# Orders of work at five places of a hybrid decoder layer: opening, key heads, MoBA's last head, third token tile, last parts of w_down

## Chip, cores and metric

The kernel runs on one core of a Trainium2 chip. The metric is the device time of one execution in microseconds (us), the median of several runs; less is better. The engines have short names: PE is TensorE (PEld its weight loads), DVE is VectorE, ACT is ScalarE, POOL is GpSimd, and SP issues most of the DMAs.

## What is computed

One layer of a decoder for 512 tokens and 1024 columns, all in float32. The width of the feed-forward part is 4096.

```python
def reference(x, p, w_in, ...):
    u = rms_norm(h, attn_pre_norm)
    gq, gk, gv, gz, gb, ga, mq, mk, mv = split(u @ w_in)
    o_gdn = gated_deltanet_group(gq, gk, gv, gz, gb, ga, conv_w, ...)   # 4 heads of 128
    o_moba = moba_group(mq, mk, mv, positions)                         # 4 heads of 128
    mix = concatenate([o_gdn, o_moba]) @ w_out
    h = h + rms_norm(mix, attn_post_norm)
    f = square(relu(rms_norm(h, mlp_pre_norm) @ w_up)) @ w_down
    h = h + rms_norm(f, mlp_post_norm)
    return h + sigmoid(h @ w_ple_gate) * (p @ w_ple)
```

The delta-rule heads (GDN) run a short convolution and SiLU over q, k and v, norm q and k, and work in chunks. A MoBA head is causal softmax attention of tiles of 128 queries; with two blocks of 256 every past block is selected.

## The kernel before

**Splitting.** Every large product is computed with operands split into a high and a low half: ACT casts the source to the high half (`L169`, `L209`, `L236`, `L749`), DVE subtracts it from the source to give the low half (`L170`, `L210`, `L237`, `L750`), and PE does three matmuls for each pair (`mm3`, `L193`). So each weight and each activation passes ACT and then DVE before PE can use it.

**Order.** Each engine runs its own queue in order. Between `L240` and `L342` (the opening) the queues of ACT, DVE and PE are in the order of the code (`tc.manual_schedule`); everywhere else a scheduler orders them by readiness and priority. SP's queue is ordered by the scheduler throughout. An instruction that waits holds up those behind it on its engine, though they may be ready.

**Opening.** The four token tiles of `x` are squared on ACT (`squares`), a root is taken on POOL, DVE scales (`normed`), PE transposes (`transpose_in`, tiles `ut`, with two PSUM buffers), and ACT and DVE split the result into `uTh` and `uTl`. Between these stand the products of `p` with `w_ple` (`embed`), whose results are copied out of PSUM (`keep`) and stored to DRAM as `ple`, and the first weight chunks `wv0` to `wv3`. `project` is the first large projection.

**Key heads.** For each of the four GDN heads `proj_conv(1, h, ...)` projects and convolves the keys into `kF`; `key_head(h)` multiplies `kF` with itself (`pkk`), transposes it (`ptk`) and computes the triangle whose inverse is then solved on DVE (`M`, from `L489`). `gdn_head(0)` follows with the queries (`pc`, `qF`, `pkq`).

**MoBA's last head.** `moba_head(3)` computes for four query tiles the scores `sc`, their softmax (`pr`; DVE scales it by the reciprocal of its sum at `L656`), the transposes `prt` on PE and the product with the values. At the same time `finish(2)` and `finish(3)` norm the outputs `u` of the last GDN heads: POOL takes a power for `so` (`L154`), DVE multiplies it (`L636`), ACT scales `u` (`L638`), and PE transposes `u` into `pot` during the gate projection `pz`.

**Third token tile.** In the loop over tiles at `L791`, the out projection of a tile (`po`) is normed, added to `x` (`L805`), and scaled (`L809`) into `xr`, from which the transposes `u2` of the next stage are made; their split is `u2Th` and `u2Tl`. The transposes of tile `t - 2` stand in the middle of tile `t`'s projection (`L798`). The first `up` products (`pu`) follow.

**The feed-forward part.** Blocks of `w_up` are multiplied (`up`, tiles `pu`), and their output goes through ReLU and square into `f`; each `f` has two sides. Three of the four groups use seven products for eight (`product`, tiles `pd`); the last group's `f` is kept split in `f_hl` (`L852`), and its parts of `w_down` are loaded and split one after another (`load_split`, `L940`), then multiplied for each token tile in `L965` and onward. Slabs of one tile row (`sf` for sources, `sr` for split halves) are taken from the front of a list and given back to its end:

```python
        def take(self):
            return self.free.pop(0)
        def give(self, *slabs):
            self.free.extend(slabs)
```

`sr.more(R_LATE, dr_)` adds twelve new slabs at the end of the list once the earlier buffers are closed. A slab's former reader must be done before it is written anew, and an instruction that waits for that holds up its queue.

Of the kernel before, what the change touches and what calls it, by code (L numbers as in the profile page):

```python
# [9 lines left out]
F32 = mybir.dt.float32  # L10
# [5 lines left out]
P = 128  # L16
# [53 lines left out]
def hybrid_layer(ctx: ExitStack, tc: tile.TileContext, x, p, w_in, w_tok, w_out, w_up, w_down, w_ple, w_gate,  # L70
# [136 lines left out]
    def put_split(dst, src):  # L207

        nc.scalar.copy(dst[0], src)  # L209
        nc.vector.tensor_sub(dst[1], src, dst[0].bitcast(F32))  # L210

    def transpose_in(u, dst, t, name, ahead=0):

        for q in range(2):
            pt = ptr(f"{name}{t}_{q}")
            for i in range(4):
                k = 4 * q + i
                nc.tensor.transpose(pt[:, i * P:(i + 1) * P], u[:, k * P:(k + 1) * P], ident)
            s = (slice(None), slice(4 * q, 4 * q + 4), slice(t * P, (t + 1) * P))
            with tc.high_priority(ahead):  # L220
                put_split((dst[0][s], dst[1][s]), j4(pt))
# [18 lines left out]
    opening = tc.manual_schedule(engines={mybir.EngineType.Activation, mybir.EngineType.DVE, mybir.EngineType.PE})  # L240
# [41 lines left out]
    def split_wv(t):  # L282
        hi, lo = split_raw(wv_raw[t], 2, 520, f"wv{t}")
        wv.extend((hi[:, i, :], lo[:, i, :]) for i in range(2))
# [53 lines left out]
    split_wv(2)  # L338
    normed(3)
    split_wv(3)  # L340
# [44 lines left out]
    def proj_conv(c, h, y):  # L385
        f = c * 4 + h
        w = load_chunk(w_in[f], P, f"w{c}{h}")
        pm = pmm(f"pc{c}{h}")
        for k in range(KT):
            mm3(pm, w[k], (uT[0][:, k, :], uT[1][:, k, :]), k == 0, k == KT - 1)  # L390
        nc.scalar.activation(y, pm, AF.Copy, scale=conv_w[:, f, 3:4])
        for i in (1, 2, 3):
            nc.vector.scalar_tensor_tensor(y[:, i:], pm[:, :T - i], conv_w[:, f, 3 - i:4 - i], y[:, i:],
                                           op0=ALU.mult, op1=ALU.add)

        th = g.tile([P, T], F32, tag="F", bufs=3, name=f"th{c}{h}")
        nc.scalar.activation(th, y, AF.Tanh, scale=0.5)
        nc.vector.scalar_tensor_tensor(y, th, 1.0, y, op0=ALU.add, op1=ALU.mult)
# [80 lines left out]
    for h in range(H):  # L479
# [5 lines left out]
        if h:  # L485
            key_head(h)


    M = g.tile([64, 2, BLK, BLK], F32, tag="M", bufs=1, name="M")  # L489
    N_, V_ = M[:, 0], M[:, 1]  # L490
    flat = lambda ap: ap.rearrange("p r c -> p (r c)")
    nc.gpsimd.memset(flat(V_), 0.0)
    nc.gpsimd.memset(flat(V_)[:, ::BLK + 1], 1.0)
    nc.sync.dma_start(flat(N_), scr.rearrange("u b r c -> (u b) (r c)"))
    for k in range(BLK - 1):
        a, b = k + 1, BLK - 1 - k
        tm = g.tile([64, a, b], F32, tag="tm", bufs=2, name=f"tm{k}")
        nc.vector.tensor_mul(tm, V_[:, :a, k:k + 1].to_broadcast([64, a, b]), N_[:, k:k + 1, a:].to_broadcast([64, a, b]))
        nc.vector.tensor_sub(V_[:, :a, a:], V_[:, :a, a:], tm)
    nc.sync.dma_start(scx[0].rearrange("u b r c -> (u b) (r c)"), flat(V_))  # L500
    nc.scalar.copy(N_.rearrange("p r c -> p c r"), V_)
    nc.sync.dma_start(scx[1].rearrange("u b r c -> (u b) (r c)"), flat(N_))
    for i in (1, 0):
        for b in range(4):
            s = slice(b * BLK, (b + 1) * BLK)
            nc.sync.dma_start(XX[i][s, :, s], scx[i, :, b].rearrange("u r c -> r u c"))
# [4 lines left out]
    def gdn_head(h):  # L511
        qf = g.tile([P, T], F32, tag="qF", bufs=3, name=f"qF{h}")
        proj_conv(0, h, qf)
# [45 lines left out]
    gdn_head(0)  # L559
# [69 lines left out]
    def finish(h):  # L629
# [6 lines left out]
        nc.vector.scalar_tensor_tensor(s, s, 0.5, rq, op0=ALU.mult, op1=ALU.mult)  # L636
# [3 lines left out]


    def moba_head(h):
        PT = g.tile([P, 4, T], F32, tag="M", bufs=1, name=f"PT{h}")
        for i in range(4):
# [11 lines left out]
            nc.vector.tensor_scalar(pr[:, :N], pr[:, :N], sum_, None, op0=ALU.mult)  # L656
# [20 lines left out]
    finish(2)  # L677
    finish(3)
# [112 lines left out]
    for t in range(NT):  # L791
# [16 lines left out]
        for i in range(2):  # L808
            nc.vector.scalar_tensor_tensor(xr[:, hf(i)], h_t[t][:, hf(i)], r, nw[1][:, hf(i)], op0=ALU.mult, op1=ALU.mult)  # L809
        nc.sync.dma_start(hd[tk(t), :], h_t[t])  # L810
        give(h_t[t])
# [21 lines left out]
    def up(b, c0, c1, between=None):  # L833
# [115 lines left out]
    give(S_s, *(sums[i] for i in (1, 7, 4)))  # L949
    C = ((sums[2], sums[3]), (sums[6], sums[5]))  # L950
# [103 lines left out]
```

## Time and profile before

| | us |
|---|---|
| median of 3 runs | 688.68 (688.54 to 688.79) |
| the profiled execution | 688.31 |
| its span on the engines | 686.5 |
| PE busy | 675.6 (98%) |
| DVE busy | 442.9 (65%) |
| ACT busy | 322.9 (47%) |
| POOL busy | 38.8 (6%) |
| granted clock of PE | 0.999 of full speed |

Times in the trace start at 0 with the span. The start of a matmul is observed, its end is modelled, so successive matmuls overlap in the rows; the distance of their starts is what one costs. The value in brackets at the end of a row is the idle time of the engine before it and what ended that.

### The profile page before, as it was taken

The numbers are of one execution on the slowest core, as the hardware profiler recorded it, in microseconds if no ns is written. First come the engines' busy times: TensorE is split into PE (matmuls) and PEld (weight loads), VectorE is DVE, ScalarE is ACT, GpSimd is POOL, SyncE is SP. The second block draws the span as 40 slices with busy tenths as digits, with TensorE's granted clock in tenths as the row PEclk, the third lists the DMA queues.
The fourth block names the chain that finished last, engine by engine and source line by source line (L and its number), as shares of the span: only waits on it lengthen the run. The fifth ranks groups of instructions, "written<-read, shape, count | busy, mean of one in ns | idle before, by whom it ended". The sixth has DMA issues, their size and how long they took to land.

```text
span 686.5 us, 8997 instructions
## 1 busy us (share of the span) xinstructions
PE 675.6 (98%) x3418; PEld 563.2 (82%) x3418; DVE 442.9 (65%) x708; ACT 322.9 (47%) x597; POOL 38.8 (6%) x72
## 2 busy tenths in 40 slices
PE   8999999999999999999999999999999999999997
PEld 6998888888877768899888888888888888788886
DVE  5759889367676655776286356956678758556632
ACT  6535343433566654555265644444444445512411
POOL 1301100000001000120000000000000000011000
PEclk9999999999999999999999999999999999999999
DMA  8831323532011117477004340154301033632431
GB/s 328 314 124 62 104 87 103 116 114 93 32 32 62 32 63 264 164 260 262 32 31 151 126 153 32 37 179 140 105 32 61 32 123 110 213 92 61 137 109 47
DMA packets 37980, 79.24 MB, mean 115 GB/s; under 512 B 9712, under 2 KB 10352, under 8 KB 37936
## 3 DMA queue, kind: packets, MB, share of 16 engines
q1 hardware_dynamic: 37360, 77.60, 34.5%
q10 hardware_dynamic: 576, 1.05, 0.5%
q8 instruction: 27, 0.44, 0.3%
q14 instruction: 17, 0.14, 0.1%
HBM read 70.51 MB, written 7.08 MB: 113 GB/s over the span
## 4 chain that ended last, share of the span: by engine, by line
PE 88%; DVE 3%; DMA 3%; ACT 2%; issue 2%; POOL 1%; ACTq 0%; DVEq 0%; POOLq 0%
PE pu L197 16%; PE pd L197 14%; PE pu L194 8%; PE pd L194 7%; PE pc L197 5%; PE pg L197 4%; PE pc L194 3%; PE po L197 3%; PE wv L197 2%; PE pg L194 2%; PE pmk L197 2%; PE pmq L197 2%; PE pz L197 2%; DMA sf<-in_w_down 1%; PE po L194 1%
## 5 line engine op out<-in xcount | busy, mean ns | idle before, releaser
L197 PE MATMUL pd<-sr,sr 128*128 128x512 f32 x464 | 143.5, 390 | 0.7 <-DVE sr L750 0.7
L197 PE MATMUL pu<-u2Tl,sr 128*128 128x512 f32 (+1 forms) x288 | 105.3, 366 | 0.5 <-DVE u2Tl L210 0.5
L194 PE MATMUL pu<-u2Th,sr 128*128 128x512 f32 (+1 forms) x288 | 105.4, 366 | 0.0
L197 PE MATMUL pu<-u2Th,sr 128*128 128x512 f32 (+1 forms) x288 | 105.2, 365 | 0.0
L197 PEld LDWEIGHTS pd<-sr,sr 128*128 128x128 f32 x464 | 87.0, 188 | 19.8 <-DVE sr L750 1.8
L194 PE MATMUL pd<-sr,sr 128*128 128x512 f32 x232 | 90.7, 391 | 0.3 <-ACT sr L749 0.3
L750 DVE TENSOR_TENSOR sr<-sf,sr 128x1024 fp32r<-128x1024 f32 x48 | 58.5, 1222 | 32.7 <-PE pd L197 13.8
L750 DVE TENSOR_TENSOR sr<-wd,sr 128x1024 fp32r<-128x1024 f32 x42 | 51.2, 1222 | 28.5 <-PE pu L197 24.3
L848 ACT ACTIVATE f<-pu 128x512 f32<-128x512 f32 (+1 forms) x36 | 19.8, 550 | 92.3 <-PE pu L197 92.3
L197 PEld LDWEIGHTS pu<-u2Tl,sr 128*128 128x128 f32 x288 | 54.3, 189 | 9.5 <-DVE u2Tl L210 0.8
L194 PEld LDWEIGHTS pu<-u2Th,sr 128*128 128x128 f32 x288 | 54.3, 189 | 8.7
L197 PEld LDWEIGHTS pu<-u2Th,sr 128*128 128x128 f32 x288 | 54.3, 188 | 8.7
L749 ACT CAST sr<-sf 128x1024 fp32r<-128x1024 f32 x48 | 50.3, 1048 | 18.5 <-DMA sf<-in_w_down 7.8
L749 ACT CAST sr<-wd 128x1024 fp32r<-128x1024 f32 x42 | 44.1, 1050 | 19.4 <-PE pd L197 19.4
L194 PEld LDWEIGHTS pd<-sr,sr 128*128 128x128 f32 x232 | 43.5, 188 | 9.8 <-ACT sr L749 1.0
L194 PE MATMUL pc<-uTh,w_h 128*128 128x512 f32 x96 | 39.0, 407 | 0.0
L197 PE MATMUL pc<-uTh,w_l 128*128 128x512 f32 x96 | 38.4, 400 | 0.0
L197 PE MATMUL pc<-uTl,w_h 128*128 128x512 f32 x96 | 38.2, 398 | 0.0
L902 DVE TENSOR_TENSOR sf<-sf,pd 128x512 f32<-128x512 f32 x28 | 19.1, 684 | 22.2 <-PE pd L197 22.2
L907 DVE TENSOR_TENSOR wd<-wd,wd 128x1024 f32<-128x1024 f32 x24 | 29.3, 1224 | 0.6
L194 PE MATMUL pg<-sr,h2Th 128*128 128x512 f32 (+1 forms) x72 | 26.5, 368 | 0.0
L197 PE MATMUL pg<-sr,h2Th 128*128 128x512 f32 (+1 forms) x72 | 26.3, 366 | 0.0
(424 smaller groups left out, 1310.3 us busy)
## 6 DMA issues: line engine op xcount, KB each, us to landing
sf<-in_w_up SPq DMA_DIRECT2D x32, 512.0 KB, 3.3
wd<-in_w_down SPq DMA_DIRECT2D x24, 512.0 KB, 4.5
w_r<-in_w_in SPq DMA_DIRECT2D x12, 512.0 KB, 3.5
wo_r<-in_w_out SPq DMA_DIRECT2D x8, 512.0 KB, 3.8
sf<-in_w_down SPq DMA_DIRECT2D x8, 512.0 KB, 4.6
sf<-in_w_ple_gate SPq DMA_DIRECT2D x8, 512.0 KB, 3.8
wv_r<-in_w_tok SPq DMA_DIRECT2D x4, 520.0 KB, 7.2
x<-in_x SPq DMA_DIRECT2D x4, 512.0 KB, 7.0
```

Source lines behind the costliest of these rows:

```text
L194: nc.tensor.matmul(dst, l[0], r[0], start=start, stop=False)
L197: nc.tensor.matmul(dst, a, b, start=False, stop=stop and i == 1)
L749: nc.scalar.copy(hi, src)
L750: nc.vector.tensor_sub(lo, src, hi.bitcast(F32))
L848: nc.scalar.activation(fq[:, side, c0:c1], pt[:, :n], AF.Relu)
L902: add(dst, dst, pts[j])
L907: sub(B[dst + (kk,)], B[x_ + (kk,)], B[y_ + (kk,)])
```

## The change

The orders are changed at five places, and nothing that is computed changes.

1. Opening. SP's queue is pinned too. `squares(0)` and `squares(1)` are moved ahead on ACT, the copy of `pl1_1` goes from DVE to ACT, the low half of a `wv` chunk is a step of its own behind the transposes' split, and the load of `wv3` with two small ones stands ahead of the stores of the second half of `ple`.
2. Key heads. `key_head(2)` and `key_head(3)` run inside `gdn_head(0)`, after the fourth of eight steps of its query projection, and the solve over `M` behind it.
3. MoBA. In `finish(2)` and `finish(3)` the last multiplication for `so` is issued behind the scaling of `pr` of tile 0 and of tile 1.
4. Third token tile. Its scaling and store are issued behind the split of the transposes of the tile before.
5. Last group. `f` is squared and split side by side and takes its slabs at side 0; the twelve late slabs are put first in the list; the load of norm 3 follows the sums.

```diff
-    opening = tc.manual_schedule(engines={mybir.EngineType.Activation, mybir.EngineType.DVE, mybir.EngineType.PE})
+    opening = tc.manual_schedule(engines={getattr(mybir.EngineType, n) for n in ("Activation", "DVE", "PE", "SP")})
...
     embed(0, 1, range(NT))
+    squares(0)
     part_of(wl, wl_in, (every, 0, hf(1)))
     part_of(wl, wl_in, (every, 1, hf(1)))
-    squares(0)
+    squares(1)
     keep(0, 0, on_s)
     keep(0, 1, on_v)
-    squares(1)
     normed(0)
...
     normed(1)
-    split_wv(0)
+    cast_wv(0)
     transpose_in(us[0], uT, 0, "ut")
-    embed(1, 1, range(2))
-    keep(1, 0, on_s)
-    keep(1, 1, on_v)
-    transpose_in(us[1], uT, 1, "ut")
-    embed(1, 1, range(2, NT))
-    split_wv(1)
+    minus_wv(0)
     wv_raw.append(load_raw(w_tok[768:1024, :], 0, 2, 520, "wv3"))
     nc.sync.dma_start(sm, small)
     nc.sync.dma_start(kc, consts[:, P:])
+    embed(1, 1, range(2))
+    keep(1, 0, on_s)
+    keep(1, 1, on_s)
+    transpose_in(us[1], uT, 1, "ut")
+    embed(1, 1, range(2, NT))
+    cast_wv(1)
+    minus_wv(1)
...
-    def proj_conv(c, h, y):
+    def proj_conv(c, h, y, at=None, between=None):
...
             mm3(pm, w[k], (uT[0][:, k, :], uT[1][:, k, :]), k == 0, k == KT - 1)
+            if k == at:
+                between()
...
-        if h:
-            key_head(h)
+        if h == 1:
+            key_head(1)
...
-    gdn_head(0)
+    def last_keys():
+        key_head(2)
+        key_head(3)
+    gdn_head(0, 3, last_keys)
+    M = g.tile([64, 2, BLK, BLK], F32, tag="M", bufs=1, name="M")
...
-    def finish(h):
+    def finish(h, after=None):
...
-        nc.vector.scalar_tensor_tensor(s, s, 0.5, rq, op0=ALU.mult, op1=ALU.mult)
+        with tc.issue_after(after) if after else ExitStack():
+            nc.vector.scalar_tensor_tensor(s, s, 0.5, rq, op0=ALU.mult, op1=ALU.mult)
...
-            nc.vector.tensor_scalar(pr[:, :N], pr[:, :N], sum_, None, op0=ALU.mult)
+            scaled[h, i] = nc.vector.tensor_scalar(pr[:, :N], pr[:, :N], sum_, None, op0=ALU.mult)
...
-    finish(2)
-    finish(3)
+    finish(2, scaled[3, 0].ins)
+    finish(3, scaled[3, 1].ins)
...
-                transpose_in(xrs[t - 2], u2T, t - 2, "u2", 60)
+                last = transpose_in(xrs[t - 2], u2T, t - 2, "u2", 60)
+                if t == 3:
+                    with tc.issue_after(last.ins):
+                        scale()
...
+        if t != 2:
+            scale()
...
-        if side:
+        if q >= NS * PAIRS:
+            if not side:
+                f_hl[q % PAIRS] = [sr.take().rearrange("p (s c) -> p s c", s=2) for _ in range(2)]
+            hi, lo = (s[:, side] for s in f_hl[q % PAIRS])
+            nc.scalar.activation(fq[:, side], fq[:, side], AF.Square)
+            nc.scalar.copy(hi, fq[:, side])
+            nc.vector.tensor_sub(lo, fq[:, side], hi.bitcast(F32))
+        elif side:
             nc.scalar.activation(fq[:, :, c0:c1], fq[:, :, c0:c1], AF.Square)
...
     sr.more(R_LATE, dr_)
-    load_norm(3)
+    sr.free = sr.free[-R_LATE:] + sr.free[:-R_LATE]
...
     give(S_s, *(sums[i] for i in (1, 7, 4)))
+    load_norm(3)
```

DVE's queue in the opening, before: `u` is the normed tile, `wv_l` the low half of a weight chunk, `uTl` the low half of the transposed tile (`ut`), `pls` a copy of a product.

```order
L280 SCALAR_TENSOR_TENSOR u_184<-x_83,r_186,nw_81 128x1024
L170 TENSOR_TENSOR wv_l<-wv_r,wv_h 128x1040
L210 TENSOR_TENSOR uTl<-ut_0_217,uTh 128x4x128
L210 TENSOR_TENSOR uTl<-ut_1_224,uTh 128x4x128
L267 COPY pls_1_240<-pl_1_200 128x512
L210 TENSOR_TENSOR uTl<-ut_0_243,uTh 128x4x128
L210 TENSOR_TENSOR uTl<-ut_1_250,uTh 128x4x128
```

After, in the same place (`wv_lo` is the low half of the chunk):

```order
L281 SCALAR_TENSOR_TENSOR u_178<-x_83,r_180,nw_81 128x1024
L210 TENSOR_TENSOR uTl<-ut_0_216,uTh 128x4x128
L210 TENSOR_TENSOR uTl<-ut_1_223,uTh 128x4x128
L291 TENSOR_TENSOR wv_lo<-wv_r,wv_hi 128x1040
L210 TENSOR_TENSOR uTl<-ut_0_247,uTh 128x4x128
L210 TENSOR_TENSOR uTl<-ut_1_254,uTh 128x4x128
```

The first pair of `uTl` moved ahead of the weight chunk's low half, and the copy between the pairs is gone from DVE.

DVE's queue at MoBA's last head, before: `pr` is the softmax of a query tile and `sum` its sum, `sc` its scores, `mx` their maximum, `so` the factors of a GDN head, `z` the gate.

```order
L636 SCALAR_TENSOR_TENSOR so_2442<-so_2442,rq_1929 128x4
L656 TENSOR_SCALAR pr_0_2377<-pr_0_2377,sum_0_2378 128x128
L648 TENSOR_TENSOR sc_1_2385<-sc_1_2385,kc 128x128
L650 TENSOR_REDUCE mx_1_2388<-sc_1_2385 128x1
L651 TENSOR_SCALAR mx_1_2388<-mx_1_2388 128x1
L633 TENSOR_TENSOR so_2460<-so_2460,rq_2111 128x4
L634 TENSOR_TENSOR so_2460<-so_2460,rq_2111 128x4
L689 SCALAR_TENSOR_TENSOR z_2597<-z_2597,pz_2572 128x512
L655 RECIPROCAL sum_1_2392<-sum_1_2392 128x1
L636 SCALAR_TENSOR_TENSOR so_2460<-so_2460,rq_2111 128x4
L691 SCALAR_TENSOR_TENSOR z_2597<-pot_2600,sm,z_2597 128x512
L656 TENSOR_SCALAR pr_1_2391<-pr_1_2391,sum_1_2392 128x256
```

After:

```order
L677 TENSOR_SCALAR pr_0_2377<-pr_0_2377,sum_0_2378 128x128
L655 SCALAR_TENSOR_TENSOR so_2442<-so_2442,rq_1929 128x4
L651 TENSOR_TENSOR so_2460<-so_2460,rq_2111 128x4
L652 TENSOR_TENSOR so_2460<-so_2460,rq_2111 128x4
L669 TENSOR_TENSOR sc_1_2385<-sc_1_2385,kc 128x128
L671 TENSOR_REDUCE mx_1_2388<-sc_1_2385 128x1
L672 TENSOR_SCALAR mx_1_2388<-mx_1_2388 128x1
L711 SCALAR_TENSOR_TENSOR z_2597<-z_2597,pz_2572 128x512
L676 RECIPROCAL sum_1_2392<-sum_1_2392 128x1
L713 SCALAR_TENSOR_TENSOR z_2597<-pot_2600,sm,z_2597 128x512
L677 TENSOR_SCALAR pr_1_2391<-pr_1_2391,sum_1_2392 128x256
L655 SCALAR_TENSOR_TENSOR so_2460<-so_2460,rq_2111 128x4
```

The scalings of `pr_0` and of `pr_1` moved ahead of the `so` of heads 2 and 3, and the two first multiplications for the second `so` now stand ahead of the scores of tile 1.

DVE's queue at the third token tile, before: `mn2r` is its norm, `sf_2665` the scaled tile, `u2Tl` the low half of the transposes of the tile before.

```order
L742 SCALAR_TENSOR_TENSOR mn2r<-mn2s,mn2r 128x1
L809 SCALAR_TENSOR_TENSOR sf_2665<-sf_2662,mn2r,sf_2659 128x512
L210 TENSOR_TENSOR u2Tl<-u_0_3030,u2Th 128x4x128
L210 TENSOR_TENSOR u2Tl<-u_1_3037,u2Th 128x4x128
L809 SCALAR_TENSOR_TENSOR sf_2665<-sf_2662,mn2r,sf_2659 128x512
```

After:

```order
L764 SCALAR_TENSOR_TENSOR mn2r<-mn2s,mn2r 128x1
L210 TENSOR_TENSOR u2Tl<-u_0_3027,u2Th 128x4x128
L210 TENSOR_TENSOR u2Tl<-u_1_3034,u2Th 128x4x128
L836 SCALAR_TENSOR_TENSOR sf_2665<-sf_2662,mn2r,sf_2659 128x512 x2
L764 SCALAR_TENSOR_TENSOR pn3r<-pn3s,pn3r 128x1
```

The first half of the scaling moved from ahead of the two `u2Tl` to behind them.

PE's queue, key head 2 and its surroundings, is changed by position alone: `pkk` of head 2 stands behind 12 matmuls of head 0's query projection (8 before), that of head 3 behind all 24 (23 before), and `pkq` of head 0 behind 4 matmuls of `pmk` (12 before). In the last group PE's first runs of `pd` were 9, 6, 2, 2, 3, 13, 7, 3, 11 and 16 matmuls of one accumulation in a row; they are now 24, 24, 24 and 24.

## Rows read from the trace of the kernel before

**Rows 1.** Page, part 1: busy us, share of the span, instructions, by engine.

```profile
PE 675.6 (98%) x3418; PEld 563.2 (82%) x3418; DVE 442.9 (65%) x708; ACT 322.9 (47%) x597; POOL 38.8 (6%) x72
```

**Rows 2.** PE's waits: engine, line, releaser: us in total, times, longest.

```profile
PE prt L659 <- DVE pr L656: 1.7, 2, 1.2
```

**Rows 3.** Timeline of PE, opening: start, us, operation, [idle before, releaser].

```profile
12.38 0.39 PE L194 MATMUL pl<-wlh,pTh 128*128 128x512 f32 x1
...
15.78 0.40 PE L197 MATMUL pl<-wll,pTh 128*128 128x512 f32 x1
17.34 1.25 PE L218 MATMUL ut<-ident,u 128*128 128x128 f32 x8 [1.16 <-DVE uTl L210]
```

**Rows 4.** Timeline of DVE, opening.

```profile
15.45 1.24 DVE L170 TENSOR_TENSOR wv_l<-wv_r,wv_h 128x1040 fp32r<-128x1040 f32 x1
16.60 1.28 DVE L210 TENSOR_TENSOR uTl<-ut,uTh 128x512 fp32r<-128x512 f32 x2
```

**Rows 5.** Timeline of ACT, opening.

```profile
11.19 0.57 ACT L267 COPY pls<-pl 128x512 f32<-128x512 f32 x1
11.66 1.06 ACT L275 ACTIVATE u<-x 128x1024 f32<-128x1024 f32 x1
```

**Rows 6.** Timeline of PE, key heads.

```profile
73.33 0.39 PE L197 MATMUL pc<-uTl,w_h 128*128 128x512 f32 x1
74.07 1.16 PE L456 MATMUL pkk<-kF 128*128 128x128 f32 x8 [0.36 <-DVE kF L398]
```

**Rows 7.** Timeline of PE, MoBA's last head.

```profile
236.23 0.39 PE L197 MATMUL pz<-uTl,wz_h 128*128 128x512 f32 x1
237.85 0.30 PE L659 MATMUL prt<-ident,pr 128*128 128x128 f32 x1 [1.23 <-DVE pr L656]
...
239.35 0.60 PE L403 MATMUL pot<-ident,u 128*128 128x128 f32 x4
...
241.87 0.40 PE L194 MATMUL pz<-uTh,wz_h 128*128 128x512 f32 x1
242.75 0.41 PE L659 MATMUL prt<-ident,pr 128*128 128x128 f32 x2 [0.48 <-DVE pr L656]
```

**Rows 8.** Timeline of DVE, MoBA's last head.

```profile
237.35 0.16 DVE L636 SCALAR_TENSOR_TENSOR so<-so,rq 128x4 f32<-128x4 f32 x1 [1.14 <-POOL so L154]
237.43 0.28 DVE L656 TENSOR_SCALAR pr<-pr,sum 128x128 f32<-128x128 f32 x1
```

**Rows 9.** Timeline of ACT, MoBA's last head.

```profile
241.70 1.28 ACT L638 ACTIVATE u<-u,so 128x128 f32<-128x128 f32 x4 [0.16 <-DVE so L636]
```

**Rows 10.** Timeline of PE, third token tile.

```profile
296.95 0.28 PE L194 MATMUL pu<-u2Th,sr 128*128 128x256 f32 x1
297.71 0.39 PE L197 MATMUL pu<-u2Tl,sr 128*128 128x256 f32 x1 [0.49 <-DVE u2Tl L210]
```

**Rows 11.** Timeline of DVE, third token tile.

```profile
296.31 0.75 DVE L809 SCALAR_TENSOR_TENSOR sf<-sf,mn2r,sf 128x512 f32<-128x512 f32 x1 [0.74 <-POOL mn2r L743]
296.98 1.28 DVE L210 TENSOR_TENSOR u2Tl<-u,u2Th 128x512 fp32r<-128x512 f32 x2
```

**Rows 12.** Timeline of PE, last products of w_down and first transposes behind.

```profile
589.08 0.39 PE L194 MATMUL pd<-sr,sr 128*128 128x512 f32 x1
...
604.18 0.39 PE L194 MATMUL pd<-sr,sr 128*128 128x512 f32 x1
...
615.74 1.03 PE L961 MATMUL h<-ident,sf 128*128 128x128 f32 x8
```

**Rows 13.** Chain that ended last: start, us, step.

```profile
583.67 1.24 DVE sr L750
584.92 4.36 DMA sf<-in_w_down
...
591.65 5.55 DMA sf<-in_w_down
```

**Rows 14.** Busy us by window: PE, PEld, DVE, ACT, POOL, clock, DMA share, GB/s.

```profile
500.00:586.00 86.00, 86.00 (x381) 71.21 (x380) 64.46 (x63) 41.56 (x46) 0.00 (x0) 1.00 0.24 80
```

More of the change, by code (lines that the diff above doesn't have):

```diff
@@ L209, in put_split @@
         nc.scalar.copy(dst[0], src)
[L210 removed]
+        return nc.vector.tensor_sub(dst[1], src, dst[0].bitcast(F32))
     def transpose_in(u, dst, t, name, ahead=0):
@@ L220, in transpose_in @@
             with tc.high_priority(ahead):
-                put_split((dst[0][s], dst[1][s]), j4(pt))
+                last = put_split((dst[0][s], dst[1][s]), j4(pt))
+        return last
     uT = split_big("uT")
@@ L280, in normed, with cast_wv, minus_wv @@
         nc.vector.scalar_tensor_tensor(us[t], x_h[t], rs[t], nw0, op0=ALU.mult, op1=ALU.mult)
-    def split_wv(t):
-        hi, lo = split_raw(wv_raw[t], 2, 520, f"wv{t}")
-        wv.extend((hi[:, i, :], lo[:, i, :]) for i in range(2))
+    wv_hl = {}
+    def cast_wv(t):
+        wv_hl[t] = [wp.tile([P, 1088], F32R, tag=n, bufs=4, name=f"wv{t}_{n}")[:, :1040] for n in ("hi", "lo")]
+        nc.scalar.copy(wv_hl[t][0], wv_raw[t][:, :1040])
+    def minus_wv(t):
+        hi, lo = wv_hl[t]
+        nc.vector.tensor_sub(lo, wv_raw[t][:, :1040], hi.bitcast(F32))
+        wv.extend((hi[:, i * 520:(i + 1) * 520], lo[:, i * 520:(i + 1) * 520]) for i in range(2))
     proj = {}
@@ L337, in hybrid_layer @@
     squares(3)
-    split_wv(2)
+    cast_wv(2)
+    minus_wv(2)
     normed(3)
-    split_wv(3)
+    cast_wv(3)
+    minus_wv(3)
     project(0, {2: lambda: transpose_in(us[2], uT, 2, "ut"), 5: lambda: transpose_in(us[3], uT, 3, "ut")})
@@ L484, in hybrid_layer, with gdn_head @@
             key_head(0)
-        if h:
-            key_head(h)
[L489 to L506, printed above, removed]
+        if h == 1:
+            key_head(1)
     u0, qF, AT, rqs, mixT = [], [], [], [], {}
-    def gdn_head(h):
+    def gdn_head(h, *other):
         qf = g.tile([P, T], F32, tag="qF", bufs=3, name=f"qF{h}")
-        proj_conv(0, h, qf)
+        proj_conv(0, h, qf, *other)
         pkq = ptr(f"pkq{h}")
@@ L557, in proj_rot @@
         return dst
-    gdn_head(0)
+    def last_keys():
[3 more added lines that the diff above has]
+    M = g.tile([64, 2, BLK, BLK], F32, tag="M", bufs=1, name="M")
+    N_, V_ = M[:, 0], M[:, 1]
+    flat = lambda ap: ap.rearrange("p r c -> p (r c)")
+    nc.gpsimd.memset(flat(V_), 0.0)
+    nc.gpsimd.memset(flat(V_)[:, ::BLK + 1], 1.0)
+    nc.sync.dma_start(flat(N_), scr.rearrange("u b r c -> (u b) (r c)"))
+    for k in range(BLK - 1):
+        a, b = k + 1, BLK - 1 - k
+        tm = g.tile([64, a, b], F32, tag="tm", bufs=2, name=f"tm{k}")
+        nc.vector.tensor_mul(tm, V_[:, :a, k:k + 1].to_broadcast([64, a, b]), N_[:, k:k + 1, a:].to_broadcast([64, a, b]))
+        nc.vector.tensor_sub(V_[:, :a, a:], V_[:, :a, a:], tm)
+    nc.sync.dma_start(scx[0].rearrange("u b r c -> (u b) (r c)"), flat(V_))
+    nc.scalar.copy(N_.rearrange("p r c -> p c r"), V_)
+    nc.sync.dma_start(scx[1].rearrange("u b r c -> (u b) (r c)"), flat(N_))
+    for i in (1, 0):
+        for b in range(4):
+            s = slice(b * BLK, (b + 1) * BLK)
+            nc.sync.dma_start(XX[i][s, :, s], scx[i, :, b].rearrange("u r c -> r u c"))
     mok, moq = proj_rot(C_MK, "mk"), proj_rot(C_MQ, "mq")
@@ L807, in hybrid_layer, with scale @@
         r = norm_r(ss, f"mn{t}")
[L808 to L811, printed above, removed]
+        def scale(t=t, xr=xr, r=r):
+            for i in range(2):
+                nc.vector.scalar_tensor_tensor(xr[:, hf(i)], h_t[t][:, hf(i)], r, nw[1][:, hf(i)], op0=ALU.mult, op1=ALU.mult)
+            nc.sync.dma_start(hd[tk(t), :], h_t[t])
+            give(h_t[t])
+        if t != 2:
+            scale()
         xrs.append(xr)
```

3 lines of the change are left out of this document (1 added, 2 removed).

## Prediction

> **What bounds the kernel now.** I began with the page's busy times [rows 1]: TensorE (PE) is busy 675.6 of 686.5 us, VectorE (DVE) 65%, ScalarE (ACT) 47%, GpSimd (POOL) 6%. So the time is PE's work plus the few places where PE stands still, and a reordering of other engines pays only there. The list of what PE waits for [rows 2] names them by line, and its largest entry is 1.7 us: no bottleneck elsewhere, only short stops. The PE timeline then gives each stop a size. I measure from start to start, because the printed ends of matmuls overlap the next starts. The pace comes from a stretch without a stop: from 604.18 to 615.74 lie 51 matmuls of 512 columns, 11.56 / 51 = 0.227 us each [rows 12]. A stop is the distance between two starts less that pace. Off these places PE runs at its pace (from 500 to 586 us it is busy 86.00 of 86.00 [rows 14]), so a stop that is removed should move everything behind it forward, all the way to the end, unless something behind it has less slack than the shift.
>
> The Trainium skill (Perfetto Trace Analysis, Identifying the Most-Contended Engine) says that matmul busy time is no measure of how near TensorE is to its limit, and that the busy share of weight loads is one; here that is 82%, which by the page would leave 18%, an estimate of 124 us, to be won. The rows speak against using it for this sum: 51 starts in a row hold one pace, so between the stops no order of other engines gives anything back.
>
> **Part 1, the opening.** PE starts a matmul at 15.78 and the transposes of token tile 1 only at 17.34, released by DVE's `uTl` [rows 3]: 1.56 - 0.23 = 1.33 us lost. DVE does the low half of the first `wv` chunk at 15.45 for 1.24 us and then the two `uTl` [rows 4], whose PSUM buffers the transposes need. The change puts the two `uTl` ahead of `wv_lo`, so they can start 1.15 us sooner (16.60 - 15.45), and gives a copy of one half tile to ACT (0.57 there, as the copy at 11.19 in [rows 5]). `normed(1)`, ahead of them, also comes earlier since `squares(0)` and `squares(1)` move up on ACT. Covers: `wv_lo` now ends one pair later (1.28), and its first reader is the projection, which PE reaches only after the 8 transposes and 6 more matmuls of 512 columns (6 x 0.227 = 1.4 us for these alone); the pinned `wv3` load stands ahead of two stores of `ple` on SP, which nobody reads before the gate stage. New cost: `keep(0, 0)`, which ran on ACT at 11.19 for 0.57 [rows 5], now stands behind `squares(1)`, a pass of 1.06 [rows 5] that ran after it, so by my count it ends near 12.4 instead of 11.76, and PE wants that bank at 12.38 [rows 3]. I price that between 0 and 0.4. Term: **1.3** (0.9 with the late bank; 1.6 if the small gap between the two halves of the transposes goes too).
>
> **Part 2, key heads.** The `pkk` matmuls of head 2 start at 74.07, 0.74 after the one before, and the releaser is DVE's `kF` [rows 6]: 0.74 - 0.23 = 0.51 lost. They move four matmuls later, 4 x 0.227 = 0.91 us, so `kF` is there. Head 3 follows all 24 matmuls instead of 23. Behind it, `pkq` of head 0 moves eight matmuls (1.8 us) earlier among those of `mk`; by my chain of ACT and DVE work `qF` is ready about 0.6 before that, so I take no cost and let it be the low end. The solve over `M` and its DMAs stand later in the program, behind head 0; by the same count it ends about 8 us before its first reader. Term: **0.5** (0 to 0.5).
>
> **Part 3, MoBA's last head.** `prt_0` starts 1.62 after the matmul before it, `prt_1` 0.88 after [rows 7]: 1.39 + 0.65 = 2.04 lost. At `prt_0` DVE has been idle for 1.14 us, waiting for POOL's power for `so`, and the ready `pr` (0.28) is queued behind that `so` [rows 8]. The change puts `pr` first. It can start where the idle time starts, 237.35 - 1.14 = 236.21, so `prt_0` moves from 237.85 to about 236.66, 1.19 earlier. But that is not the whole story. `pot`, at 239.35 [rows 7], reads `u`, which is scaled with the same `so`. POOL's chain is untouched, so `so` still ends at 237.5, ACT's four scalings take 1.28 [rows 9] and end near 238.85. PE, four matmuls behind `prt_0`, would want the first at 238.16 and the last at about 238.5. So only some 0.7 of the gain survives up to there. Then comes `prt_1`: `so` of the next head is moved behind its `pr`, `prt_1` was 3.40 behind `pot` of which 0.65 was waiting, and `pr_1` is ready by my chain (`z` on ACT, `z` twice on DVE, `pr`) about 0.1 before PE arrives. Term: 0.7 + 0.65 = **1.3** (0.65 if `prt_1` still waits; 2.0 if both go whole).
>
> **Part 4, third token tile.** PE starts a `pu` at 296.95 and the next at 297.71, released by `u2Tl` [rows 10]. These have 256 columns and go at 0.12: 0.64 lost. DVE did a scaling of 0.75 (296.31) ahead of the two `u2Tl` (296.98) [rows 11]. It waited for POOL before that, and the scaling now follows the pair. So the pair starts about 0.7 to 1.4 us sooner. The scaled tile is read by transposes that stand behind 36 more matmuls of 256 columns (36 x 0.12 = 4.3 us), and its store goes out behind it, so the delay of 1.3 is covered. Term: **0.65** (0.5 to 0.75).
>
> **Part 5, the last parts of `w_down`.** From 589.08 to 604.18 PE starts 57 matmuls [rows 12]: 15.10 - 57 x 0.227 = 2.18 us lost, in three stops and in switches between accumulation groups that the scheduler made to fill them. The chain of waits shows why: loads of `w_down` issued at 584.92 and 591.65 took 4.36 and 5.55 to land and were each followed by ACT's cast and DVE's subtraction of 1.24 [rows 13]. The low and high halves took slabs first in, first out, behind the last `up` blocks, while twelve new ones lay at the end of the list. Now the twelve come first, `norm` 3 loads later, and `f` is squared and split by sides, so half of it is done a block earlier. By a count with the same durations the fourth part is ready about 4 us before PE wants it, the last about 3, and the last side of `f` about 1.1. Extra work: four more pairs of smaller operations. Two subtractions of 512 columns cost 1.28 [rows 11] against 1.24 for one of 1024, so this is below 0.1 each and lies on DVE beside PE's 24-matmul runs. PE's switches go too (four plain runs of 24). Term: **2.0** (0.8 if the last side of `f` or a late part still stops PE; 2.2 at most).
>
> **Sum.** 1.3 + 0.5 + 1.3 + 0.65 + 2.0 = 5.75. The profiled execution took 688.31 (span 686.5 and 1.8 around it): 688.31 - 5.75 = 682.6. It lies 0.37 below the median of 688.68, so I predict a median of 682.9. The low ends sum to 0.9 + 0 + 0.65 + 0.5 + 0.8 = 2.85, the high ends to 7.05: 685.8 and 681.6.
>
> **Rivals.** (a) *Slower, by the slabs.* `f`'s slabs are now taken at side 0, one product and one `up` block (48 matmuls, 10.9 us) before they were. Two slabs fewer are free in the third group (512 to 589). If each of the seven last products then waits for one subtraction of 1.22, that is +8.5 against -5.75: 691.4. It decides from 0.8 us per product. Against it: PE loses nothing there now [rows 14], and by my count of slab returns the tightest part keeps about 1 us. 4%.
> (b) *The stops move.* In parts 1 and 3 DVE is freed, but ACT or POOL comes last instead: the opening's casts and bank, `so` and `z` in MoBA. Then these two give 0.9 + 0.65 less, and with 0.5 of small new stops behind the shift 3.7 remain: 685.0. For it: the margins of 0.1 and 0 named above. Against it: the other three parts don't share them. 17%.
> (c) *The last parts stay bound by the transfers.* The loads of the last parts still share one queue with those of the gate's weights. If they land as late as the two shown [rows 13], part 5 gives 0.8 or less: 684.1. Against it: the first of these loads takes the norm's place at the head of SP's queue, and all follow sooner. 10%. The Trainium skill (DMA: Bandwidth & Descriptors, Issuing engines are not separate DMA queues) says that all transfers run on the same 16 engines and interleave; by it earlier loads lengthen their neighbours, which would make (c) likelier. No run here shows the new order yet.
> (d) *The pins hold nothing.* If the orders change but the same data come last, the time stays: 688.7. The stated order of DVE does change at these places, so 2%.
>
> **How the numbers follow.** The forecast has 67%. The range reaches to (b) and (c) and to the bounds: 681.8 to 686.0. A difference of 0.2% (1.4 us) is about what a measurement can tell from none. Faster: forecast, (b), (c) and most of what is between, 94%. Same: (d) and half-failed mixes, 2%. Slower: (a), 4%.
>
> **What would show it.** Right: `ut` of tile 1 starting one pace after the matmul before it; `pkk` of head 2 without a wait; `pr` of the last head's first tile on DVE ahead of `so`, `pot` then waiting for `u` by about half a microsecond; the `pu` pair at 0.12; four runs of 24 at the end at 0.227. Wrong: PE waits between 512 and 589 us, or stops of new names at the old places; then the time lies at the upper end or above it.

## The result and the profile after

The changed kernel takes **682.64 us** (median of 6 runs, 681.66 to 683.32) against 688.61 of the kernel before beside it: ratio 0.9913, with a 95% interval of 0.9901 to 0.9926. It is faster by 5.97 us; 682.9 was predicted. The profiled execution took 682.94, 1.7 more than its span of 681.2 (before: 686.5).

The page of the kernel after, part 1 (busy us, share, instructions) and the first line of part 4 (the chain that ended last, shares by engine):

```profile
PE 674.9 (99%) x3418; PEld 564.1 (83%) x3418; DVE 442.9 (65%) x711; ACT 324.5 (48%) x606; POOL 39.3 (6%) x72
...
PE 98%; DMA 1%; DVE 1%; ACT 0%; issue 0%; ACTq 0%
```

Against [rows 1], PE has nearly the same busy time (675.6 there) in a span that is 5.3 shorter. PE's waits after (engine, line, releaser: us in total, times, longest):

```profile
PE pwarm L246 <- DVE warm L243: 1.4, 1, 1.4
PE pu L197 <- DVE u2Tl L210: 0.3, 1, 0.3
```

The `prt` entry of [rows 2] is gone and so is all else but the warm-up at the start, which both kernels have, and one wait for `u2Tl`, at a place where the kernel before had none. These are the places of the prediction, in the timeline of PE after (start, us, operation, [idle before, releaser]):

```profile
14.16 0.39 PE L197 MATMUL pl<-wll,pTh 128*128 128x512 f32 x1
...
16.41 0.40 PE L197 MATMUL pl<-wll,pTh 128*128 128x512 f32 x1
16.65 1.03 PE L218 MATMUL ut<-ident,u 128*128 128x128 f32 x8
...
73.05 0.39 PE L197 MATMUL pc<-uTh,w_l 128*128 128x512 f32 x1
73.28 1.05 PE L471 MATMUL pkk<-kF 128*128 128x128 f32 x8
...
234.55 0.39 PE L197 MATMUL pz<-uTl,wz_h 128*128 128x512 f32 x1
234.99 0.30 PE L680 MATMUL prt<-ident,pr 128*128 128x128 f32 x1
...
236.48 1.12 PE L418 MATMUL pot<-ident,u 128*128 128x128 f32 x4
...
239.53 0.40 PE L194 MATMUL pz<-uTh,wz_h 128*128 128x512 f32 x1
239.77 0.38 PE L680 MATMUL prt<-ident,pr 128*128 128x128 f32 x2
...
293.95 0.28 PE L194 MATMUL pu<-u2Th,sr 128*128 128x256 f32 x1
294.06 0.28 PE L197 MATMUL pu<-u2Tl,sr 128*128 128x256 f32 x1
...
307.18 0.28 PE L194 MATMUL pu<-u2Th,sr 128*128 128x256 f32 x1
307.75 0.39 PE L197 MATMUL pu<-u2Tl,sr 128*128 128x256 f32 x1 [0.29 <-DVE u2Tl L210]
...
585.89 0.39 PE L194 MATMUL pd<-sr,sr 128*128 128x512 f32 x1
...
610.37 1.03 PE L997 MATMUL h<-ident,sf 128*128 128x128 f32 x8
```

`ut` of tile 1 starts 0.24 after the matmul before it (1.56 in [rows 3]), `pkk` 0.23 (0.74 in [rows 6]), `prt_0` 0.44 and `prt_1` 0.24 (1.62 and 0.88 in [rows 7]), the `pu` pair 0.11 (0.76 in [rows 10]). The four `pot` take 1.12 where they took 0.60: PE waits for `u` inside them. At 307.75 stands the new stop. From 585.89 to 610.37 lie 108 matmuls: 24.48 / 108 = 0.227, so the last products run at pace throughout; before, the same stretch took 26.66 [rows 12].

DVE and ACT at MoBA's last head, after, explain both `prt_0` and `pot`; here are two rows of DVE's timeline and one of ACT's:

```profile
234.55 0.28 DVE L677 TENSOR_SCALAR pr<-pr,sum 128x128 f32<-128x128 f32 x1
235.74 0.17 DVE L655 SCALAR_TENSOR_TENSOR so<-so,rq 128x4 f32<-128x4 f32 x1 [0.90 <-POOL so L154]
...
235.94 1.28 ACT L657 ACTIVATE u<-u,so 128x128 f32<-128x128 f32 x4 [0.35 <-DVE so L655]
```

DVE still idles before `so`, waiting for POOL as in [rows 8], but `pr` no longer stands behind it. `so` itself is not earlier relative to its neighbours, so ACT ends `u` at 237.2, and `pot` has to wait.

And the windows of the stretch behind the new stop (us; busy PE, PEld, DVE, ACT, POOL with their instructions; clock; DMA share; GB/s):

```profile
307.75:586.00 278.25, 278.25 (x1272) 232.34 (x1273) 184.43 (x182) 139.20 (x178) 0.00 (x0) 1.00 0.32 105
```

PE is busy all of it, which includes the third group of products, where the prediction's slower case was to show stops.

### The profile page after: what moved, and what is told of

Read it like the earlier page. It is cut to its first block, busy times and chain, and to the rows that moved or that the text cites. A ratio compares the mean times of both kernels' runs of the same rounds, so it can differ in the third digit from the quotient of the medians.

```text
span 681.2 us, 9010 instructions
## 1 busy us (share of the span) xinstructions
PE 674.9 (99%) x3418; PEld 564.1 (83%) x3418; DVE 442.9 (65%) x711; ACT 324.5 (48%) x606; POOL 39.3 (6%) x72
## 3 DMA queue, kind: packets, MB, share of 16 engines
q10 hardware_dynamic: 576, 1.05, 0.5%
## 4 chain that ended last, share of the span: by engine, by line
PE 98%; DMA 1%; DVE 1%; ACT 0%; issue 0%; ACTq 0%
PE pu L197 16%; PE pd L197 15%; PE pu L194 8%; PE pd L194 8%; PE pc L197 6%; PE pg L197 4%; PE po L197 4%; PE pc L194 3%; PE wv L197 2%; PE pz L197 2%; PE pg L194 2%; PE po L194 2%; PE pmk L197 2%; PE pmq L197 2%; PE pav L684 1%; PE sc L668 1%
## 5 line engine op out<-in xcount | busy, mean ns | idle before, releaser
L194 PE MATMUL pg<-sr,h2Th 128*128 128x512 f32 (+1 forms) x72 | 26.5, 368 | 0.0
L197 PE MATMUL pg<-sr,h2Tl 128*128 128x512 f32 (+1 forms) x72 | 26.3, 366 | 0.0
```

What stands on the lines that cost most here:

```text
L194: nc.tensor.matmul(dst, l[0], r[0], start=start, stop=False)
L197: nc.tensor.matmul(dst, a, b, start=False, stop=stop and i == 1)
```

## Where the 5.3 us of the span came from

Both kernels issue the same 3418 matmuls, so the start of each can be set against the start of the matmul with the same number before. This difference keeps a level between two places and steps at each place where PE lost or won time:

| place | step of the level, us | predicted |
|---|---|---|
| first matmuls of `pl`, start | +0.64 | - |
| opening, `ut` of tile 1 | -1.56 | -1.3 (0.9 to 1.6) |
| `ptk` of key head 0, at 55 | -0.26 | - |
| key heads, `pkk` of head 2 | -0.63 | -0.5 (0 to 0.5) |
| `ks`, at 178 | +0.13 | - |
| MoBA's last head | -1.33 | -1.3 (0.65 to 2.0) |
| third token tile | -0.74 | -0.65 (0.5 to 0.75) |
| `u2Tl` at 307 | +0.56 | - |
| last parts of `w_down` | -2.18 | -2.0 (0.8 to 2.2) |
| sum | -5.37 | -5.75 |

The five terms sum to 6.44 against 5.75 predicted. Four further steps, together +1.07, were not in the sum. One of them, the start, differs between executions of the same code (see below); without it the steps come to 6.01, near the 5.97 between the medians.

## Experiments: each part alone

Each of five kernels is the kernel before with one part of the change alone.

**Part 1, the opening.** Edit in short:

```diff
-    split_wv(0)
+    cast_wv(0)
     transpose_in(us[0], uT, 0, "ut")
+    minus_wv(0)
```

> The kernel before with the opening's orders alone (SP pinned, squares earlier, the first two uTl ahead of the low half of wv0). Theory (DVE's order is what stopped the transposes of token tile 1): the stop of 1.33 us at the second ut goes, nothing new comes, so about 1.3 to 1.5 off 688.6, that is 687.1 to 687.3, and PE's other stops keep their sizes. Rival (ACT or POOL is last there): a stop of 0.4 to 0.9 stays at the same ut, 687.8 to 688.2.

687.29 against 688.67, ratio 0.9973 (0.9964 to 0.9983): 1.38 faster. In its trace `ut` of tile 1 starts 0.23 behind the matmul before it, and the list of PE's waits no longer has `ut` nor `ptk`. That list of the kernel before has a line that the prediction didn't use:

```profile
PE ptk L403 <- DVE kF L398: 0.3, 1, 0.3
```

It is the unforeseen step at 55. `p2_keys` below still has this wait; `p1_opening` has not. So it belongs to the opening, 38 us ahead of it: there DVE's wait for the high half of the weights ahead of `kF` is 0.39 instead of 0.71. That PE's other stops would keep their sizes was wrong: `ptk` went, and further down 0.5 of the gain is given back, since the stops at the last parts of `w_down`, which this kernel still has, are larger when PE arrives sooner.

**Part 2, key heads.**

```diff
+    def last_keys():
+        key_head(2)
+        key_head(3)
+    gdn_head(0, 3, last_keys)
```

> The kernel before with the key heads alone moved into the query projection of head 0, the solve over M behind it. Theory: the stop of 0.52 at pkk of head 2 goes and pkq of head 0, eight matmuls earlier, does not wait: 688.1. Rival: pkq waits for qF by about half a microsecond and the time stays at 688.6.

688.03, ratio 0.9987 (0.9976 to 0.9998): 0.64 faster. `pkk` starts 0.23 after its neighbour. `pkq` and the later solve over `M` show no wait, so their cost of nothing held. Head 3's `pkk` has a small loss that the prediction didn't count: it starts 0.38 behind its neighbour (0.23 before), and its second matmul 0.21 behind the first (0.11 before).

**Part 3, MoBA's last head.**

```diff
+    finish(2, scaled[3, 0].ins)
+    finish(3, scaled[3, 1].ins)
```

> The kernel before with the two so multiplications alone issued behind the scaling of pr. Theory: prt_0 starts 1.2 earlier, pot then waits about 0.4 to 0.5 for u, whose so still ends when POOL's power does, prt_1 no longer waits (0.65): 1.3 off, 687.3. Rival 1: u is there as early as pot, 2.0 off, 686.6. Rival 2: prt_1 still waits, 0.7 off, 687.9.

687.27, ratio 0.998 (0.997 to 0.9989): 1.4 faster. The excess over pace at `prt_0` fell from 1.39 to 0.21, that at `prt_1` from 0.65 to 0, and the four `pot` take 1.11 instead of 0.60.

**Part 4, third token tile.**

```diff
+                if t == 3:
+                    with tc.issue_after(last.ins):
+                        scale()
```

> The kernel before with the scaling of token tile 2 alone issued behind the split of tile 1's transposes. The profile of the whole change shows the stop of 0.64 at pu gone, but a new one of 0.45 ten microseconds later, at a pu that waits for u2Tl of tile 3, behind the low half of a weight block whose load landed late. Theory: removing the stop brings the load of that block closer to two loads of w_down issued 2.4 us before the stop, it lands 0.7 to 0.8 later against PE, and the new stop belongs to this part: it appears here too, 0.3 to 0.45, and only 0.2 to 0.3 is won, 688.3. Rival: the late landing was an accident of one execution or of the other parts; no new stop here, 0.65 won, 688.0.

688.41, ratio 0.9992 (0.9983 to 1.0002): by the times alone not told apart from no change. The trace tells why: the pair at 297 is at pace, and the stop that the kernel after has at 307 is here too. PE's timeline of this kernel:

```profile
310.56 0.28 PE L194 MATMUL pu<-u2Th,sr 128*128 128x256 f32 x1
311.08 0.39 PE L197 MATMUL pu<-u2Tl,sr 128*128 128x256 f32 x1 [0.24 <-DVE u2Tl L210]
```

0.52 less the pace of 0.12 is 0.40, and with the start behind it, late by another 0.10, it takes back 0.50 of the 0.74 that the part wins. The stop needs none of the other four parts. Nor does it always need this one: `only_s` (below), which lacks part 4, loses 0.21 at the same matmul.

**Part 5, the last parts.**

> The kernel before with the last group's changes alone (late slabs first, norm 3 later, f squared and split by sides). Theory: all of the 2.18 us lost from 589 to 604 goes, 2.0 to 2.2 off 688.6, so 686.4 to 686.6, and no PE stop appears from 512 to 589. Rival (slabs of f taken a block earlier are short): stops in the third group, 688 or above.

686.45 against 688.95, ratio 0.9964 (0.9949 to 0.9979): 2.5 faster, with no stop of PE in the last products. Added up, the five kernels give 1.38 + 0.64 + 1.4 + 0.26 + 2.5 = 6.2, near the 5.97 of all together; each of these differences is uncertain by 0.6 to 1.0 (half its interval), so that no more can be read from the sum.

## Experiments: the two halves of part 5

Part 5 has two edits: `f` by sides, and the late slabs first in the list together with the later `norm`. One kernel has the first alone (`only_f`), one the second (`only_s`).

```diff
+            hi, lo = (s[:, side] for s in f_hl[q % PAIRS])
+            nc.scalar.activation(fq[:, side], fq[:, side], AF.Square)
```

> The kernel before with f squared and split by sides alone; slabs in the old order, norm 3 where it was. Theory (the parts of w_down were late because of their slabs and transfers, f only a little): the stop that ACT's cast of f ends (0.48) goes, those that the parts end (0.33 and 0.69) stay, 0.3 to 0.7 off: 688.0 to 688.3. Rival (f's full-width square, cast and subtraction hold up the parts' casts in ACT's queue): 1.5 or more off, 687.1 or below.

```diff
+    sr.free = sr.free[-R_LATE:] + sr.free[:-R_LATE]
```

> The kernel before with the late slabs first and norm 3 later, f split whole as before. Theory: the parts are in time, the stop at f's last whole split stays (0.5 to 0.8), so 1.3 to 1.6 off: 687.0 to 687.3. Rival: f's whole split holds the parts' casts, only 0.5 off, 688.1.

`only_f`: 688.38, ratio 0.9997 (0.9985 to 1.0009). `only_s`: 688.77, ratio 0.9998 (0.9988 to 1.0008), where 687.0 to 687.3 was expected: wrong. Neither half alone gains anything that can be measured. The chain of waits of `only_f` (start, us, step):

```profile
592.29 5.17 DMA sf<-in_w_down
...
597.49 1.05 ACT sr L749
598.54 0.62 ACT qn00j L734 x2
599.16 0.94 ACT sr L749
...
600.14 0.50 PE pd L194
```

In place of the three stops of the kernel before stands a single large one of 1.31 here, and what comes last is a part of `w_down` whose load was issued late, at 592.29. The chain of `only_s`:

```profile
588.54 5.41 DMA sf<-in_w_down
...
593.97 2.00 ACT sr L749 x2
...
596.02 0.50 PE pd L194
```

Here that load is issued 3.8 us sooner, yet a stop of 1.67 remains: two casts stand in one row on ACT, the first that of the late part, the second that of the whole of `f`. `f` had been squared before, but its cast is queued behind one that waits for the DMA. So two things came last close to each other, and taking away one shows the other; the 2 us come only with both. This is what the prediction's low end of 0.8 stood for ("if the last side of `f` or a late part still stops PE"), and each half alone gave even less than that.

## Experiments: the new stop at 307

The chain of waits of the kernel after, at the stop:

```profile
299.33 5.45 DMA sf<-in_w_up
...
304.79 1.05 ACT sr L771
...
305.87 1.23 DVE sr L772
307.10 0.61 DVE u2Tl L210
...
307.75 0.50 PE pu L197 x2
```

A `w_up` block lands, ACT casts it, DVE subtracts, and `u2Tl`, which needs nothing of this block, stands behind that subtraction on DVE. Before, the same load was issued at 303.07 and took 4.63, and nobody waited. SP's timeline and PE's, before:

```profile
303.07 0.34 SPq L786 DMA_DIRECT2D sf<-in_w_up  x1
```

```profile
310.92 0.28 PE L194 MATMUL pu<-u2Th,sr 128*128 128x256 f32 x1
```

PE starts the matmul ahead of this place 7.85 after the load's issue in both kernels (310.92 - 303.07 and 307.18 - 299.33): the issue moved forward with PE, so the microseconds won upstream took nothing from this load's slack. What differs is how long the load took. Two things can be varied: DVE's order, and the load, which goes out behind two loads of `w_down` (issued 293.91 and 294.34) that had not landed.

**DVE's order** (`fix_u2_dve`): the low half of that block is issued behind the split of the fourth token tile.

```diff
-        nc.vector.tensor_sub(lo, src, hi.bitcast(F32))
+        with tc.issue_after(after) if after else ExitStack():
+            nc.vector.tensor_sub(lo, src, hi.bitcast(F32))
```

> The changed kernel with one more order: on DVE the low half of the weight block that is read two up blocks later is issued behind the split of token tile 3's transposes. Theory (that low half ahead of u2Tl is what makes the new stop of 0.45): the stop shrinks to under 0.1, 0.35 to 0.45 better than the changed kernel, 682.2. Rival (ACT's cast ahead of u2Th is late as well): half of it stays, 682.4.

682.12, ratio 0.9901 (0.9886 to 0.9917); the stop is gone from the trace and no new one stands behind it. But in this execution the load took only 4.76, behind the same two unfinished loads of `w_down`, so the trace alone doesn't show that it was the order that removed the stop.

**The load** (`wd_after`): the eight loads of the first group's `w_down` rows are issued behind the `w_up` load, DVE's order left alone. The changed kernel ran beside it once more.

```diff
+            with tc.issue_after(ld[3].ins) if g == 0 else ExitStack():
+                B[r, c, kk] = load_rows2(raw_d[i], w_down[:, hf(c)], HB * r + PAIRS * g + 2 * kk)
```

> The changed kernel, but all eight loads of the first group's w_down rows are issued behind the load of the third w_up block that is loaded in the loop, the one whose landing (5.45 us after its issue) decides the stop of 0.45 us at 307. Theory, that this load came late because two w_down loads were under way beside it: it lands in 4.6 us or less, the ACT cast, DVE's subtraction and u2Tl come 0.8 us earlier, and the stop shrinks to 0.1 us or nothing, without any change to DVE's order; 682.2 to 682.4 us, if the w_down loads, now later by 5 to 8 us, are still in time (their first reader is far behind). Rival, that the load is late because its own issue was released late, or because the DMA engines are full in any case: it still takes over 5 us and the stop stays at 0.4.

> The changed kernel once more, beside three variants of it, so that differences of a few tenths of a microsecond are read side by side. Every theory expects what it gave before, 682.6 us, and the same stops of TensorE: about 0.45 us at 307 (the fourth token tile of the w_up product) and two of about 0.18 us at 236.7 and 237.0 (pot waiting for u).

`after_again` took 682.86 (682.35 to 683.25), ratio 0.9914 (0.99 to 0.9929), with a stop of 0.51 at the same place; its load took 5.50. `wd_after` took 682.18, ratio 0.9907 (0.9891 to 0.9924). The DMA view of `wd_after` from 298.5 to 303.5 (issues: KB each, median us from issue to landing), and the cast in ACT's timeline:

```profile
sf<-in_w_up SPq DMA_DIRECT2D x1, 512.0 KB, 4.7
```

```profile
303.40 1.05 ACT L771 CAST sr<-sf 128x1024 fp32r<-128x1024 f32 x1 [2.29 <-DMA sf<-in_w_up]
```

The load lands in 4.75, not quite the 4.6 expected but 0.7 less than in the kernel after, and PE runs through that place at pace. The size of the stop follows the load's time. In the traces of the kernels that keep DVE's order, that is:

| kernel | load took, us | PE over its pace, us |
|---|---|---|
| `after_again` | 5.50 | 0.51 |
| the kernel after | 5.45 | 0.45 |
| `p4_tile` | 5.39 | 0.40 |
| `only_s` | 5.20 | 0.21 |
| `hold2` (below) | 5.11 | 0.13 |
| `wd_after`, the kernel before and five others | 4.33 to 4.75 | 0 |

The line through these meets no stop at just under 5 us. `best` (below) has the new order on DVE and a load of 5.24, for which this line gives about 0.25, an estimate; it has no stop at this place. So the stop needs both, a load of over 5 us and DVE's order.

Why the load is late in some executions stays open. It is not shown to be the two loads of `w_down`: `fix_u2_dve` has them unfinished in front as the kernel after has, and its load took 4.76; and in `wd_after` another `w_up` load, issued 0.8 earlier, was unfinished in their place. Part 4 seems to make a late load likelier. It brings the second of the `w_down` loads from 5.7 to 5.0 ahead of this one, and the load took 4.76 to 5.50 in the six kernels with part 4 and this order of loads, 4.33 to 5.20 in the seven without part 4; the ranges overlap, with one traced execution of each kernel. The Trainium skill (DMA: Bandwidth & Descriptors, Issuing engines are not separate DMA queues) says that all transfers run on the same engines and interleave; no run here shows that it was this that lengthened the load. The prediction used that sentence for the last parts only, where it changed nothing, and not here.

## Experiments: the slabs, and one more order

**The slabs** (`hold2`): the changed kernel with two slabs out of use through the third group, the last that has seven products.

```diff
+        if g == NS - 1:
+            held = [sr.take(), sr.take()]
```

> The changed kernel with two of the sr slabs taken out of use before the last group and given back behind it; nothing that is computed changes. It prices the prediction's rival of a shortage of slabs. Theory of the prediction (a count: about 1 us of slack where late slabs are asked for): with two slabs fewer the parts of a product are cast only when the product before has freed its slabs, and TensorE stops by up to 1.2 us at most of the seven products, 3 to 8 us in all, 686 to 691 us. Rival, that slabs were never near short: stops of less than 0.3 us in the last group and 682.6 to 683.2 us.

685.0 against 682.86, ratio to the kernel before 0.9948 (0.9933 to 0.9963). PE's timeline has two stops that the kernel after lacks:

```profile
563.64 0.39 PE L197 MATMUL pu<-u2Tl,sr 128*128 128x512 f32 x1
564.82 0.50 PE L197 MATMUL pu<-u2Th,sr 128*128 128x512 f32 x1 [0.79 <-DVE sr L772]
...
591.20 0.39 PE L194 MATMUL pd<-sr,sr 128*128 128x512 f32 x1
592.40 0.50 PE L194 MATMUL pd<-sr,sr 128*128 128x512 f32 x1 [0.81 <-ACT sr L884]
```

They are 0.95 and 0.97 over pace, 1.9 together; the first lies in the third group, the second behind it, in the last. Neither theory held as put: the slabs are not far from short, since two fewer do stop PE, but it stops at two places and not at most of seven products. At the first, the subtraction that PE wants stands on DVE behind an addition that waits for PE's own product; whether it also lacked its slab until then the rows don't tell.

**One more order** (`best`): on top of `fix_u2_dve`, head 2's four `pot` stand three matmuls later.

```diff
+            if h == 3 and k == 0:
+                gate(2, pz_2)
```

> The changed kernel with two more orders: DVE makes the low half of the third w_up block's weights behind the split of the fourth token tile instead of ahead of it (as in fix_u2_dve), and head 2's four matmuls of pot stand three matmuls later, behind the first of head 3's gate product. Theory, that each of TensorE's remaining stops is one instruction behind the wrong neighbour: the stop at 307 (0.45 us) and the two at 237 (0.37 us together) are both gone and nothing takes their place; 681.7 to 681.9 us, 0.7 to 0.9 below the changed kernel. Rival, that a stop taken away only shows the next: one of the two is there again elsewhere and it is 682.1 to 682.4 us.

682.43, ratio 0.9906 (0.9891 to 0.9921). The rival's price held. The four `pot` take 0.35 instead of 0.88 from their start to that of the next matmul (0.53 won; the 0.37 of the expectation counted only the two longest gaps), and `prt_1` stops in its place; PE's timeline, and the end of the chain that released it:

```profile
238.26 0.40 PE L194 MATMUL pz<-uTh,wz_h 128*128 128x512 f32 x1
238.96 0.41 PE L680 MATMUL prt<-ident,pr 128*128 128x128 f32 x2 [0.30 <-DVE so L655]
```

```profile
236.48 0.49 ACT z L705
...
237.00 0.69 DVE z L706
...
237.80 0.14 DVE z L708
...
238.47 0.34 DVE pr L677
```

The chain `z`, `z`, `z`, `pr` is as late as before, and PE now reaches `prt_1` 0.47 too soon (0.70 between the two starts, less 0.23). So its margin in the changed kernel was 0.06, the 0.53 won less that 0.47, as small as the 0.1 that the prediction had counted, and it was the wait of `pot` that paid for it.

Of the three variants none can be told from another by its time (682.12, 682.18, 682.43), and against the changed kernel (682.64 and 682.86) the intervals overlap. That none of them stops at 307 rests on the traces, and only in `best` was the load late enough for DVE's order to matter.

## Why the prediction was right

**What bounds the kernel.** "A stop that is removed should move everything behind it forward": the difference stays at 3.19 from 308 to 586. That held because PE is at pace in between; the weight loads' 82% of [rows 1] became 83%, and what was won came from the stops alone.

**The terms.** All five came out above the forecast, by 0.03 to 0.26 and by 0.69 together; only part 2 lies above its high end (0.63 against 0.5). The prediction sized a stop as "the distance between two starts less that pace", and this leaves out that the start behind the stop is late as well. At the third token tile, before, the matmul behind the one at 297.71 [rows 10] starts 0.22 later where the pace is 0.12:

```profile
297.94 0.28 PE L197 MATMUL pu<-u2Th,sr 128*128 128x256 f32 x1
```

That is 0.10 of the 0.74 won there, and `pkk` of head 2 has the same 0.10. In the opening the excess is the gap between the two halves of the transposes (0.16), which the high end of 1.6 had allowed for. The last parts gave back all of the 2.18 that the prediction had counted there, of which it had taken 2.0. The late bank of `keep(0, 0)`, which was to cost up to 0.4, cost nothing: from the third `pl` to the transposes PE keeps one distance to the kernel before, 0.62 to 0.65 in the kernel after and at most 0.06 in `p1_opening`. Part 3 was right in its inner step as well: 1.18 won at `prt_0`, of which `pot` takes back 0.53 (half a microsecond was forecast), then 0.65 won at `prt_1`.

**What the sum lacked.** Four steps. Without the start they come to +0.43, which hides most of the 0.69 by which the terms fell short: that 682.9 lies so near to 682.64 is in part luck.
- The start, +0.64, which is not of the change. Half of it (0.30) is there at the first `pl`, as the first load of `w_ple` landed at 4.55 instead of 4.25; the rest is PE's clock. The trace's record of the granted clock begins, at its full level, at 5.61 in the kernel before, at 6.65 in the kernel after and at 4.90 in `wd_after`; the `pl` ahead of that start 0.43 or more apart, those soon behind it 0.23, about what the lower of its two levels (1.2 GHz) and then the upper one (2.4 GHz) would make of 512 columns. What PE did until then, from 1.44 on, are the six matmuls of the warm-up and the first of `pl`. In PE's timeline of the kernel after and of `wd_after`, in this order, the first matmuls show it: four starts take 1.50 in the one and 1.05 in the other, and the second row is 0.60 later.

```profile
5.60 1.67 PE L264 MATMUL pl<-wlh,pTh 128*128 128x512 f32 x4
7.10 1.09 PE L264 MATMUL pl<-wlh,pTl 128*128 128x512 f32 x4
```

```profile
5.45 1.21 PE L264 MATMUL pl<-wlh,pTh 128*128 128x512 f32 x4
6.50 1.09 PE L264 MATMUL pl<-wlh,pTl 128*128 128x512 f32 x4
```

  Before, the stop of 1.33 at `ut` took up most of such a difference. In the seven traces that keep that stop its size goes from 0.67 to 1.45, smaller where the first matmuls are late, and the projection begins at 19.83 to 20.27 in all of them. In the seven with the new opening it begins at 18.19 to 19.01, and the difference goes to the end.
- `ptk`, -0.26, was in the list of waits and was not assigned to a part.
- `ks` at 178, +0.13, appears with the opening's change alone too (`p1_opening`).
- The stop at 307, +0.56 (0.45 and, at the start behind it, 0.10). The prediction's own condition, "unless something behind it has less slack than the shift", was checked for the instructions that the change moves, and not for a load 10 us further on; and it was not the shift that used up the slack there, but a load that took 5.45 instead of 4.63.

**The rivals.** (a) *Slower, by the slabs* didn't happen, and `hold2` shows it was mispriced: with another two slabs fewer PE loses 2, not 8.5, which still leaves it 3.8 faster than before. As a mechanism it was real; as a case on the slower side it was not. (b) Its mechanism is in the trace twice (the wait at `pot`, and DVE's order at 307) but at 0.53 and 0.56, and only `best` shows the full exchange of one stop for another. (c) is refuted for the whole change by the last load, which is issued at 585.79 and lands at 590.45, where [rows 13] has 591.65 and 5.55 for one of them; with half of part 5 it is what happens. (d) is refuted at all five places.

## What to carry to other kernels

When one engine is at its pace between short stops, measure each stop from start to start, the start behind it included, and assign every line of the list of waits to a part of the change, the smallest too. A stop whose inputs come by two paths that end close together goes only when both are moved, so try the halves before calling one of them useless. A microsecond won at one stop is taken from the slack of what doesn't move with it, as `best` showed at `prt_1`: look there for the next stop. A load whose issue moves with PE keeps its slack, but its time differs between executions, so an instruction queued behind work on that load, which it doesn't need itself, stops the kernel in some of them. And take a step that differs between executions of the same code out of the account before praising or blaming the change.

## What the runs showed that was not expected

The same load of 512 KB, behind the same two unfinished loads, landed in 4.76 us in one execution and in 5.45 to 5.50 in others; from just under 5 us on, what it lost was lost by PE. PE's granted clock reached its full level 4.90 us into the span in one execution and 6.65 in another of the same opening, and the first `pl` went at about half the pace until then. The stop at `ut` had evened out most of that; without it the projection begins up to 0.8 us apart from one execution to the next. And the start behind a stop came about 0.10 late as well.
